# The selected-attention branch of eight decode samples, reordered by phase: keys of both groups first, then values of both groups

## The chip, the cores and the metric

The kernel runs on one core of a Trainium2 chip. The metric is the device time of one execution in microseconds; lower is better. The kernel before has a median of 1252.27 us over three runs (1243.72 to 1252.75).

## The reference

One layer of a hybrid decoder is run for a prompt of 512 tokens and for eight decode samples of four tokens each, with 2048 cached positions behind each sample. The layer is: x plus the output projection of two mixers (a sparse attention called NSA, and an mLSTM), plus cross-attention on a memory, plus a SwiGLU, with RMS norms between. The part that matters here is NSA for the samples, `nsa_attend` in the reference, with 8 heads in 2 key/value groups of width 64:

```python
# compressed branch: scores on compressed keys, softmax, weights on compressed values
# the compressed weights, summed over blocks and heads, rank 32 blocks of 64 tokens; the best 16 are kept
# selected branch: scores on all cached keys, positions outside the kept blocks masked, softmax, values
# window branch: the same over the last 512 positions
out = gate_cmp * o_cmp + gate_slc * o_slc + gate_win * o_win
y = concat(headnorm(out), sigmoid(o) * headnorm(mlstm)) @ w_out
```

The comments in this extract sum up the code. The cached keys and values are gathered through a page table. Every sample has its own pages, so no key or value is shared by two samples.

## The kernel before

All work of a phase of the layer is issued by Python generators that are woven together, and a scheduler in the framework then fixes the order of every engine's instructions from its own estimate of times. The chip runs each engine's list in order; what an instruction waits for is a semaphore of the instruction or transfer that makes its data or frees its buffer.

The stretch that the change touches lies in the middle of the program. In the background runs `compress(1)`, the small MLP that makes compressed values (in the profile the matmuls at L218 to L220 into `bd` and L1296 into `xa`, then L1246 and L1216). Woven into it is the chain `fg`, in which `sample()` is the third part and `open_late()` the last. When `compress(1)` is through, `drain(fg)` runs the rest, and `early_mix()` splits the NSA and mLSTM outputs `oF` into two parts (`mh`, `ml`) for the output projection of the first 272 tokens. That projection is 192 matmuls, in four column chunks of `w_out`, each chunk loaded by three DMAs (L1830, L1832) and split by ScalarE and VectorE into `whi` and `wlo` (L213, L214). A second part of it, on the other 272 tokens, reads `hh` and `hl`.

`sample()` handles the eight samples in two groups `g` of four. For the selected branch, each group goes through these steps:

- weights of the compressed branch: a `quad` of four matmuls against `kcT`, minimum on VectorE, an Exp (L1607) and block sums on VectorE;
- keys: `half` issues four indirect gathers of 512 KB on GpSimd's queue (L573), one for each sample, and each covers half of that sample's keys. `keys` transposes 128 by 512 elements with four TensorE transposes into one of two PSUM banks `tp` (L1517), and `evac` moves them to `kt` (L206 on ScalarE three times of four, L208 on VectorE once);
- selection: a transpose and a matmul (L1624, L1627), the top 16 blocks on VectorE as a mask `mk`, and the mask added to the bias on GpSimd (`M4`, L1642);
- four score chunks: a `quad` (L1527), then VectorE adds the mask and takes the minimum while it moves the scores to `SS` (L1653); between chunks the keys of the next chunk are transposed;
- softmax: four Exp of 128x512 on ScalarE (L1672) and one small one (L1674);
- values: `probs` transposes the weights through the same two `tp` banks to `PTs`, and 64 matmuls (L1693) add weights times gathered values into `po`.

After group 0, and ahead of group 1, `finals_p` finishes the prompt's NSA: the compressed attention is added (L1398, L1401), the squares (L1402) go through a matmul with `bones` (L1407), and a Ln (L1408) and an Exp (L1413) on ScalarE give the norm's factor. The gathered tiles `gat` have eight buffers. A gather waits until the tile that held its buffer has been read for the last time. The gathers go in the order keys(0), values(0), keys(1), values(1), each in two halves. The last two value tiles of group 1 use other buffers and are loaded early.

Of the kernel before, what the change touches and what calls it, by code (L numbers as in the profile page):

```python
# [6 lines left out]
F32 = mybir.dt.float32  # L7
# [29 lines left out]
def body(tc, I, O, stage=99, dbg=None):  # L37
    nc = tc.nc
    with ExitStack() as top:
# [1351 lines left out]
        def finals_p(var):  # L1391
            yield from need(("p", 1))
            var = var[:, :2048].rearrange("p (a b n) -> p a b n", a=2, b=2)
            for j in range(5):
                if j < 4:
                    acc = bank(psp)
                    for v in range(2):
                        nc.tensor.matmul(acc[64 * v:64 * v + 64], vcP[32 * j:32 * j + 32, v], PcT[32 * j:32 * j + 32, v],  # L1398
                                         start=True, stop=True)
                    oj = oF[:, j, :512]  # L1400
                    nc.vector.tensor_tensor(oj, oj, acc, op=OP.add)  # L1401
                    nc.scalar.activation(var[:, j // 2, j % 2], oj, AF.Square)  # L1402
# [12 lines left out]
            yield  # L1415

        def sample():
# [175 lines left out]

            kg = half("cache_k_slc", 0, 0)
            for g in range(2):
                bs = [4 * g + q for q in range(4)]
                rs = sc.tile([128, 4], F32, name="rs4", bufs=2)
                nmn = sc.tile([128, 12], F32, name="nmn", bufs=2)
                kh = half("cache_k_slc", g, 1, range(3))
                yield from need(("c", 0))  # L1600
                pc = bank(psp)
# [15 lines left out]
                nc.vector.scalar_tensor_tensor(blk, edge, 0.5, blk, op0=OP.mult, op1=OP.add)  # L1617
                yield
                kts = [keys(lambda i: kg[q][:, 128 * i:128 * i + 128]) for q in range(2)]
                yield  # L1620
                kts += [keys(lambda i: kg[q][:, 128 * i:128 * i + 128]) for q in range(2, 4)]
                yield
                p = bank(ptp)
# [12 lines left out]
                nc.vector.match_replace(out=ia, in_to_replace=t8[:, 8:16], in_values=ia, imm_value=-BIG)  # L1636
                mk = sc.tile([128, 32], F32, name="mk")
                nc.vector.memset(mk, 0.0)
                nc.vector.tensor_scalar(mk[:, 1:31], ia, -0.5 * BIG, BIG, op0=OP.is_ge, op1=OP.mult)
                M4 = sc.tile([128, 4, 128], F32, name="M4")  # L1640
                for i in range(4):
                    nc.gpsimd.tensor_tensor(M4[:, i].rearrange("p (j r) -> p j r", r=4),  # L1642
                                            B0[:, i].rearrange("p (j r) -> p j r", r=4),
                                            mk[:, :, None].to_broadcast([128, 32, 4]), op=OP.add)
                kh += half("cache_k_slc", g, 1, (3,))
                yield
                yield
                yield
                SS = sc.tile([128, 2080], F32, name="SS")
                for c in range(4):  # L1650
# [4 lines left out]
                    if c == 3:  # L1655
                        break
                    src = kg if c == 0 else kh
# [17 lines left out]
                nc.vector.tensor_reduce(rs[:, 1:2], bs5[:, 5:10], axis=AX.X, op=OP.add)  # L1675
                nx = 2 * g
                vl = half("cache_v_slc", g, 1, range(4 - nx))
                yield
                yield
                if nx:  # L1680
                    yield from need("free")
                    vl += half("cache_v_slc", g, 1, range(4 - nx, 4), True)
                PT_ = probs(lambda i: SS[:, 128 * i:128 * i + 128])
                yield
                po_ = bank(ppo)
                for c in range(4):
                    vg = vh if c < 2 else vl
                    if c < 3:
# [7 lines left out]
                    if c == 0:  # L1696
# [3 lines left out]
                        nc.vector.tensor_copy(PN_, p[:32, 0:128])  # L1700
                    if c == 2 and g == 0:
                        kg = half("cache_k_slc", 1, 0)
                    yield
# [5 lines left out]
                if g == 0:  # L1709
                    yield from finals_p(sc.tile([128, 2080], F32, name="SS"))  # L1710
            pop("sc")
# [874 lines left out]
```

## Time and profile before

| | before |
|---|---|
| three runs, us | 1243.72, 1252.75, 1252.27 |
| median, us | 1252.27 |
| the profiled execution: time, us | 1244.16 |
| the profiled execution: span, us | 1242.4 |
| TensorE busy, share of the span | 95% |
| granted TensorE clock, mean | 0.972 |

The profiled execution is close to the fastest of the three runs; the two others lie some 8.5 us above it. The stretch in question begins near 500 us of the span and ends near 630 us. Times in the rows below are microseconds from the start of the span.

### The profile page before, as it was taken

How to read it: one execution, taken by the hardware profiler on the slowest of the kernel's cores; microseconds unless marked ns; L12 is line 12 of the kernel's file. 1: busy time of each engine (PE TensorE's matmuls, PEld its weight loads, DVE VectorE, ACT ScalarE, POOL GpSimd, SP SyncE). 2: the span in 40 equal slices, each digit the busy share in tenths (PEclk: the TensorE clock that was granted, in tenths of full speed). 3: DMA queues.
4: the chain of work that ended last, by engine and by line, in shares of the span. 5: the costliest groups of instructions: out<-in, count | busy, mean ns of one | idle time of the engine just before them, and what ended most of it. 6: DMA issues, size and time to landing. Idle time of an engine off the chain costs nothing.

```text
span 1242.4 us, 24591 instructions
## 1 busy us (share of the span) xinstructions
PE 1174.2 (95%) x9220; PEld 1066.4 (86%) x9220; DVE 830.3 (67%) x1901; ACT 615.7 (50%) x1418; POOL 564.0 (45%) x686
## 2 busy tenths in 40 slices
PE   7999999899997989988899998999999999999996
PEld 5998999588885879846699977599899999999996
DVE  6336683567887787544566575544987887878874
ACT  5235665745646434474543233433575565565452
POOL 1013353566766366442243100034796586486442
PEclk9998999989997989998899999999999999999998
DMA  7324240141253184585468399650023322322411
GB/s 232 102 53 104 86 152 1 53 135 43 74 175 115 57 294 152 176 276 154 122 168 179 111 221 278 233 169 2 1 100 105 103 94 96 118 94 77 137 52 73
DMA packets 141769, 154.30 MB, mean 124 GB/s; under 512 B 17449, under 2 KB 123689, under 8 KB 141394
## 3 DMA queue, kind: packets, MB, share of 16 engines
q1 hardware_dynamic: 131922, 119.17, 32.1%
q0 software_dynamic: 9728, 33.56, 8.3%
q8 instruction: 73, 1.20, 0.4%
q14 instruction: 46, 0.38, 0.1%
HBM read 141.67 MB, written 13.12 MB: 125 GB/s over the span
## 4 chain that ended last, share of the span: by engine, by line
PE 53%; DVE 7%; DMA 5%; ACT 2%; issue 1%; POOL 1%; SPq 1%; POOLq 0%; DVEq 0%; ACTq 0%
PE xc L2260 7%; PE xa L2260 7%; PE bd L2260 6%; PE tp L2260 5%; PE bd L218 3%; PE bd L220 3%; PE bd L219 3%; PE xa L1296 2%; DMA wraw<-in_w_out 2%; DMA mkv<-in_cache_mem_k 2%; PE tp L1517 1%; PE bd L2159 1%; PE xc L218 1%; PE xc L219 1%; PE xc L220 1%
## 5 line engine op out<-in xcount | busy, mean ns | idle before, releaser
L214 POOL TENSOR_TENSOR al<-fraw,ah 128x512 fp32r<-128x512 f32 (+1 forms) x104 | 127.1, 1224 | 146.8 <-ACT ah L213 118.9
L213 ACT ACTIVATE whi<-wraw 128x1024 fp32r<-128x1024 f32 (+3 forms) x74 | 63.0, 890 | 70.1 <-DMA wraw<-in_w_xv 28.4
L214 DVE TENSOR_TENSOR wlo<-wraw,whi 128x1024 fp32r<-128x1024 f32 (+3 forms) x74 | 75.0, 1041 | 31.2 <-ACT whi L213 31.0
L213 ACT ACTIVATE ah<-fraw 128x512 fp32r<-128x512 f32 (+1 forms) x112 | 66.0, 594 | 43.8 <-PE xc L2260 11.8
L218 PE MATMUL bd<-w1h,xh 128*128 128x256 f32 x256 | 82.9, 326 | 0.0
L1198 POOL TENSOR_TENSOR xs<-xf 128x256 f32<-128x256 f32 x64 | 57.3, 902 | 48.5 <-PE xa L1296 29.7
L220 PE MATMUL bd<-w1h,xl 128*128 128x256 f32 x256 | 75.7, 298 | 1.4 <-DVE xl L214 1.4
L219 PE MATMUL bd<-w1l,xh 128*128 128x256 f32 x256 | 76.1, 298 | 0.0
L1296 PE MATMUL xa<-ws,xs 128*128 128x256 f32 x256 | 70.9, 399 | 1.9 <-DVE bq L1469 1.0
L625 POOL TENSOR_SCALAR sb<-sb,rs,gat 128x128 f32<-128x128 f32 (+3 forms) x64 | 46.2, 726 | 56.0 <-DVE rs L624 41.9
L213 ACT ACTIVATE xh<-xf 128x512 fp32r<-128x512 f32 x64 | 40.1, 632 | 43.6 <-DVE xf L1191 19.8
L213 ACT ACTIVATE ah<-sp 128x512 fp32r<-128x512 f32 (+1 forms) x64 | 35.6, 557 | 41.6 <-DVE sp L2200 16.9
L1191 DVE STREAM_TRANSPOSE xf<-cgat 128x512 f32<-128x512 f32 x64 | 44.9, 704 | 15.8 <-POOL xs L1198 15.0
L220 PEld LDWEIGHTS bd<-w1h,xl 128*128 128x128 f32 x256 | 49.1, 192 | 5.4 <-DVE xl L214 2.8
L219 PEld LDWEIGHTS bd<-w1l,xh 128*128 128x128 f32 x256 | 49.8, 195 | 4.3 <-issue 3.0
L214 DVE TENSOR_TENSOR xl<-xf,xh 128x512 fp32r<-128x512 f32 x64 | 48.2, 757 | 7.2 <-ACT xh L213 6.7
L1296 PEld LDWEIGHTS xa<-ws,xs 128*128 128x128 f32 x256 | 45.8, 198 | 8.1 <-issue 3.0
L218 PEld LDWEIGHTS bd<-w1h,xh 128*128 128x128 f32 x256 | 49.5, 195 | 3.7 <-issue 2.2
L219 PE MATMUL bd<-hlo,whi 128*128 128x272 f32 x176 | 52.4, 298 | 0.0
L218 PE MATMUL bd<-hhi,whi 128*128 128x272 f32 x176 | 52.2, 297 | 0.0
L220 PE MATMUL bd<-hhi,wlo 128*128 128x272 f32 x176 | 51.9, 295 | 0.0
L1874 POOL TENSOR_TENSOR acc<-acc,sq 128x272 f32<-128x272 f32 x35 | 31.4, 896 | 34.3 <-ACT sq L1873 33.9
(988 smaller groups left out, 4672.6 us busy)
## 6 DMA issues: line engine op xcount, KB each, us to landing
fraw<-in_w_gate SPq DMA_DIRECT2D x11, 1024.0 KB
fraw<-in_w_up SPq DMA_DIRECT2D x11, 1024.0 KB
fraw<-in_w_down SPq DMA_DIRECT2D x24, 384.0 KB
mkv<-in_cache_mem_k SPq DMA_DIRECT2D x64, 128.0 KB
mkv<-in_cache_mem_v SPq DMA_DIRECT2D x16, 512.0 KB
wraw<-in_w_in SPq DMA_DIRECT2D x8, 512.0 KB
wraw<-in_w_xq SPq DMA_DIRECT2D x4, 1024.0 KB
wraw<-in_w_xk SPq DMA_DIRECT2D x4, 1024.0 KB
```

What stands on the lines that cost most here:

```text
L213: nc.scalar.activation(hi, src, AF.Copy)
L214: (eng or nc.gpsimd).tensor_tensor(lo, src, hi, op=OP.subtract)
L218: nc.tensor.matmul(out, ah, bh, start=first, stop=False, **kw)
L219: nc.tensor.matmul(out, ah, bl, start=False, stop=False, **kw)
L220: nc.tensor.matmul(out, al, bh, start=False, stop=last, **kw)
L625: (nc.vector, nc.gpsimd)[1].tensor_scalar(sb[:, :n], sb[:, :n], rs, gat[:, i, 3 * h + 1 + br:3 * h + 2 + br], op0=OP.mult, op1=OP.mult)
L1191: nc.vector.transpose(xf.rearrange("p a (q i) -> p q a i", q=4), gs[0].rearrange("p (q t a i) -> p t q a i", q=4, t=4, a=4)[:, t])
L1198: nc.gpsimd.tensor_tensor(xs_.rearrange("p c (v j) -> p v c j", v=2), xg[:, 0], xg[:, 1], op=OP.add)
L1296: nc.tensor.matmul(dst[2], ops[2][:, kk], w1s[t][2][:, kk], start=t == 0 and kk == 0, stop=t == 3 and kk == 1, skip_group_check=True)
L1517: nc.tensor.transpose(p[:, 128 * i:128 * i + 128], srcs(i), ident)
L1874: nc.gpsimd.tensor_tensor(acc[hf], acc[hf], sq, op=OP.add)
L2260: nc.tensor.matmul(p[:, :HALF], w[a][:, k], x[b_][:, k], start=first and k == 0 and i == 0, stop=last and k == n - 1 and i == 2, skip_grou ...
```

## The change

Only `sample()` and `finals_p` change. The gathers, transposes, matmuls and exponentials stay the same in number; four Ln and four Exp of 128x512 in `finals_p` become four copies, one Ln and one Exp of 128x2048. The body of `sample()` is cut into `weigh(g)` and `select(g)`, and the two groups go keys, keys, values, values. Group 1's `weigh` and `select` stand between the score chunks of group 0. The scores `SS` get two buffers, and group 1's mask goes into another tile (`W0`). The gathers now go in the order keys(0), keys(1), values(0), values(1). `finals_p` follows the values of group 0, as before.

```diff
@@ finals_p
-                    nc.scalar.activation(vj, p, AF.Ln, bias=eps_t)
+                    nc.scalar.activation(vj, p, AF.Copy)
...
+            nc.scalar.activation(var, var, AF.Ln, bias=eps_t)
+            nc.scalar.activation(var, var, AF.Exp, scale=-0.5)
             for j in range(4):
                 oj, vj = oF[:, j, :512], var[:, j // 2, j % 2]
-                tc.keep_in_program_order(nc.scalar.activation(vj, vj, AF.Exp, scale=-0.5))
@@ sample
+            G, st_ = {}, {}
+            G[0, "k0"] = half("cache_k_slc", 0, 0)
+            G[0, "k1"] = half("cache_k_slc", 0, 1, range(3))
+            for g in range(2):
...
+                if g == 0:
+                    yield from need(("c", 0))
+                    weigh(0)
                 yield
+                kts = [keys(lambda i: G[g, "k0"][q][:, 128 * i:128 * i + 128]) for q in range(2)]
...
+                if g == 0:
+                    select(0)
+                M4 = sc.tile([128, 4, 128], F32, name=("M4", "W0")[g])
...
-                SS = sc.tile([128, 2080], F32, name="SS")
+                SS = sc.tile([128, 2080], F32, name="SS", bufs=2)
                 for c in range(4):
...
+                    if g == 0 and c > 0:
+                        (weigh, select)[c - 1](1)
+                    if c == 2:
+                        if g == 0:
+                            G[1, "k1"] = half("cache_k_slc", 1, 1)
+                        else:
+                            G[0, "v1"] = half("cache_v_slc", 0, 1)
                     if c == 0:
-                        vh = half("cache_v_slc", g, 0)
+                        if g == 0:
+                            G[0, "k1"] += half("cache_k_slc", 0, 1, (3,))
+                            G[1, "k0"] = half("cache_k_slc", 1, 0)
+                        else:
+                            G[0, "v0"] = half("cache_v_slc", 0, 0)
...
-                vl = half("cache_v_slc", g, 1, range(4 - nx))
+                st_[g] = SS, rs
                 yield
+            for g in range(2):
+                SS, rs = st_[g]
+                if g:
                     yield from need("free")
+                    G[1, "v1"] += half("cache_v_slc", 1, 1, range(2, 4), True)
...
+                    if c == 1 and g == 0:
+                        G[1, "v0"] = half("cache_v_slc", 1, 0)
+                    if c == 3 and g == 0:
+                        G[1, "v1"] = half("cache_v_slc", 1, 1, range(2))
```

Lines after the change are numbered higher: L1518 for L1517, L1528 for L1527, L1626 for L1627, L1660 for L1642, L1701 for L1672, L1722 for L1693. The change moves instructions on every engine. Three places follow.

**TensorE, keys of group 1.** Before, at the second score chunk of group 1 (`sp<-kt,Qn` is a `quad`, `tp<-ident,gat` a key transpose, `xc<-mh,whi` and its like are output projection):

```order
L218 MATMUL xc<-mh,whi 128x272
L219 MATMUL xc<-ml,whi 128x272
L1527 MATMUL sp<-kt,Qn 32x512 x4
L1517 MATMUL tp<-ident,gat 128x128 x4
L220 MATMUL xc<-mh,wlo 128x272
```

With the change, from the selection of group 1 (L1626) on, through the last chunk of group 0 and the first two of group 1:

```order
L1626 MATMUL tp<-blk,GS 128x32
L1528 MATMUL sp<-kt,Qn 32x512 x4
L1518 MATMUL tp<-ident,gat 128x128 x8
L1246 MATMUL xc<-w_5309,hid 127x64 x4
L1518 MATMUL tp<-ident,gat 128x128 x8
L1216 MATMUL xc<-ident,ys 128x128 x4
L1518 MATMUL tp<-ident,gat 128x128 x4
L1528 MATMUL sp<-kt,Qn 32x512 x4
L1518 MATMUL tp<-ident,gat 128x128 x16
L1528 MATMUL sp<-kt,Qn 32x512 x4
```

All output-projection matmuls now stand behind the value matmuls of group 0, and all but four behind those of group 1. In the key phase only L1246 and L1216 of `compress(1)` stand between the transposes.

**ScalarE, the norms of `finals_p`.** Before (`pcs` is group 1's `weigh`, `kt` its keys):

```order
L1408 ACT_TABLE_LOAD
L1408 ACTIVATE SS<-tp,eps_t 128x512 x2
L1607 ACT_TABLE_LOAD
L1607 ACTIVATE pcs,rs_6684<-pcs,nmn 128x127
L1408 ACT_TABLE_LOAD
L1408 ACTIVATE SS<-tp,eps_t 128x512
L213 ACTIVATE mh<-oF 128x272 x4
L1408 ACTIVATE SS<-tp,eps_t 128x512
L1413 ACT_TABLE_LOAD
L1413 ACTIVATE SS<-SS 128x512 x3
L206 ACTIVATE kt<-tp 128x512
L1413 ACTIVATE SS<-SS 128x512
```

With the change (`PTs` are the transposed weights of group 1's values):

```order
L1402 ACTIVATE SS<-oF 128x512
L1408 ACTIVATE SS<-tp 128x512
L1758 ACTIVATE jkn,rs_7401<-po_3201 128x128
L1408 ACTIVATE SS<-tp 128x512
L1411 ACT_TABLE_LOAD
L1411 ACTIVATE SS<-SS,eps_t 128x2048
L206 ACTIVATE PTs<-tp 128x512 x2
L1412 ACT_TABLE_LOAD
L1412 ACTIVATE SS<-SS 128x2048
L206 ACTIVATE PTs<-tp 128x512
L213 ACTIVATE mh<-oF 128x272
```

Four table loads are now two, and what stands behind them is group 1's weights for the values, no longer its keys. The softmax of group 0 (L1701), which stood ahead of `finals_p`, now stands among the key evacuations of group 1.

**GpSimd's queue, the gathers.** Before, from the first values of group 0 on:

```order
L573 DMA gat<-in_cache_v_slc,gx 128x1024
L1642 TENSOR_TENSOR M_6046<-B_5476,mk 128x128 x4
L573 DMA gat<-in_cache_v_slc,gx 128x1024
L1198 TENSOR_TENSOR xs<-xf 128x2x2x64
L573 DMA gat<-in_cache_v_slc,gx 128x1024 x2
L1198 TENSOR_TENSOR xs<-xf 128x2x2x64
L573 DMA gat<-in_cache_v_slc,gx 128x1024 x4
L573 DMA gat<-in_cache_k_slc,gx 128x1024 x8
L214 TENSOR_TENSOR ml<-oF,mh 128x272 x4
L573 DMA gat<-in_cache_v_slc,gx 128x1024
L1642 TENSOR_TENSOR M_6809<-B_5476,mk 128x128 x4
L573 DMA gat<-in_cache_v_slc,gx 128x1024 x5
```

With the change, the same stretch:

```order
L573 DMA gat<-in_cache_k_slc,gx 128x1024
L1660 TENSOR_TENSOR M_6048<-B_5476,mk 128x128 x4
L573 DMA gat<-in_cache_k_slc,gx 128x1024
L1198 TENSOR_TENSOR xs<-xf 128x2x2x64
L573 DMA gat<-in_cache_k_slc,gx 128x1024 x2
L1198 TENSOR_TENSOR xs<-xf 128x2x2x64
L573 DMA gat<-in_cache_k_slc,gx 128x1024 x4
L1660 TENSOR_TENSOR W_6421<-B_5476,mk 128x128 x4
L573 DMA gat<-in_cache_v_slc,gx 128x1024 x4
L214 TENSOR_TENSOR ml<-oF,mh 128x272 x2
L573 DMA gat<-in_cache_v_slc,gx 128x1024 x10
```

All value gathers stand behind all key gathers, and behind the mask of group 1 (`W`).

On SyncE, the loads of `w_out`'s first three chunks keep their place; the fourth stood right behind the third, and now stands behind the sample's x, two later `w_out` loads and the first load of `w_xq`.

## Rows read from the trace of the kernel before

**Rows 1.** The profile page, its first two parts: the span, TensorE's busy share in 40 slices of 31 us, in tenths (the stretch in question is slices 18 to 20).

```profile
span 1242.4 us, 24591 instructions
...
PE   7999999899997989988899998999999999999996
```

**Rows 2.** The view by stretches of time. Columns: the stretch, its length, then busy us and instructions of TensorE, its weight loads, VectorE, ScalarE and GpSimd, then the granted TensorE clock as a share of 2.4 GHz, the share of the DMA engines, GB/s.

```profile
552.30:568.00 15.70, 9.26 (x31) 3.67 (x30) 10.96 (x23) 14.45 (x26) 4.75 (x6) 0.67 0.38 135
568.00:582.00 14.00, 14.00 (x114) 13.01 (x114) 4.34 (x12) 2.75 (x4) 5.31 (x8) 1.00 0.86 265
...
595.00:611.00 16.00, 13.49 (x184) 9.50 (x177) 5.99 (x27) 8.57 (x24) 1.75 (x3) 0.79 0.04 10
...
640.00:860.00 220.00, 213.53 (x1679) 188.11 (x1679) 127.82 (x248) 79.44 (x165) 47.17 (x67) 1.00 0.65 178
533.60:627.40 93.80, 78.89 (x695) 57.05 (x695) 47.43 (x119) 53.52 (x108) 26.07 (x31) 0.89 0.60 188
609.70:627.40 17.70, 16.44 (x139) 15.48 (x135) 14.50 (x38) 9.52 (x23) 5.93 (x8) 1.00 0.92 247
```

**Rows 3.** The view of waits, TensorE, 530 to 611 us: instruction and tile, what ended the wait, us in total, times, the longest.

```profile
PE tp L1517 <- ACT kt L206: 6.6, 3, 2.8
PE tp L1517 <- ACT SS L1408: 2.8, 2, 1.6
```

**Rows 4.** The timeline of TensorE: start, us, instruction, and in brackets the idle time before it and what ended that.

```profile
545.64 1.08 PE L1693 MATMUL po<-gat,PTs 128*32 128x128 f32 x32
...
555.01 0.66 PE L1517 MATMUL tp<-ident,gat 128*128 128x128 f32 x4 [1.65 <-ACT SS L1408]
...
560.33 2.12 PE L1517 MATMUL tp<-ident,gat 128*128 128x128 f32 x8 [2.81 <-ACT kt L206]
...
568.42 0.37 PE L218 MATMUL xa<-mh,whi 128*128 128x272 f32 x1
...
569.51 0.29 PE L220 MATMUL xa<-mh,wlo 128*128 128x272 f32 x1
...
571.03 0.29 PE L219 MATMUL bd<-ml,whi 128*128 128x272 f32 x1
571.16 1.03 PE L1517 MATMUL tp<-ident,gat 128*128 128x128 f32 x8
...
588.11 0.43 PE L220 MATMUL bd<-mh,wlo 128*128 128x272 f32 x1
...
594.38 1.06 PE L1527 MATMUL sp<-kt,Qn 128*32 128x512 f32 x8 [0.69 <-ACT kt L206]
...
601.78 1.94 PE L1693 MATMUL po<-gat,PTs 128*32 128x128 f32 x32
...
627.44 0.40 PE L218 MATMUL xa<-hh,whi 128*128 128x272 f32 x1
```

**Rows 5.** The timeline of ScalarE, same columns: the norms of `finals_p`, splits for the output projection, and the softmax of group 1.

```profile
547.13 1.28 ACT L1408 ACT_TABLE_LOAD   x1
548.42 0.69 ACT L1408 ACTIVATE SS<-tp,eps_t 128x512 f32<-128x512 f32 x1
...
554.86 1.38 ACT L213 ACTIVATE mh<-oF 128x272 fp32r<-128x272 f32 x4
...
556.83 1.28 ACT L1413 ACT_TABLE_LOAD   x1
558.12 1.67 ACT L1413 ACTIVATE SS<-SS 128x512 f32<-128x512 f32 x3
559.70 0.58 ACT L206 ACTIVATE kt<-tp 128x512 f32<-128x512 f32 x1
...
563.88 2.00 ACT L213 ACTIVATE whi<-cgat 128x1024 fp32r<-128x1024 f32 x2
...
596.67 0.32 ACT L1674 ACTIVATE SS<-sn,nmn 128x32 f32<-128x32 f32 x1 [2.34 <-DVE nmn L1668]
...
599.11 0.71 ACT L1672 ACTIVATE SS<-SS,bs 128x512 f32<-128x512 f32 x1
```

**Rows 6.** The view by lines, TensorE, 533.5 to 627.4 us, shapes apart: line, operation, tiles, shapes, times, then busy us in all and mean ns of one, and the idle time before.

```profile
L1693 PE MATMUL po<-gat,PTs 128*32 128x128 f32 x224 | 11.8, 304 | 0.0
L1517 PE MATMUL tp<-ident,gat 128*128 128x128 f32 x64 | 11.0, 309 | 9.5 <-ACT kt L206 6.6 <-ACT SS L1408 2.8
...
L1517 PE MATMUL tp<-ident,SS 128*128 128x128 f32 x32 | 6.8, 323 | 0.1
...
L1407 PE MATMUL tp<-SS,bones 128*128 128x512 f32 x8 | 4.4, 632 | 0.0
L1398 PE MATMUL sp<-PcT,vcP 32*64 32x512 f32 x16 | 4.3, 613 | 0.2 <-DVE oF L1401 0.2
```

**Rows 7.** The view of DMA issues in the stretches 568 to 578 and 589 to 593 us: tile and source, queue, times, median us from issue to landing.

```profile
gat<-in_cache_v_slc,gx POOLq DMA_INDIRECT x4, 8.3
...
gat<-in_cache_v_slc,gx POOLq DMA_INDIRECT x2, 5.1
```

**Rows 8.** The chain of waits that ended last, in order of time (start, us, what): the third and fourth chunk of `w_out`.

```profile
570.21 12.30 DMA wraw<-in_w_out
...
583.63 1.23 DVE wlo L214
...
586.18 4.75 DMA wraw<-in_w_out
```

More of the change, by code (lines that the diff above doesn't have):

```diff
@@ L1592, in half, with weigh @@
                 return r
-            kg = half("cache_k_slc", 0, 0)
-            for g in range(2):
+            sel = {}
+            def weigh(g):
                 bs = [4 * g + q for q in range(4)]
[L1597 to L1600, printed above, removed]
+                rs = sc.tile([128, 4], F32, name="rsc")
+                nmn = sc.tile([128, 1], F32, name="nmc")
                 pc = bank(psp)
@@ L1617, in sample, with select @@
                 nc.vector.scalar_tensor_tensor(blk, edge, 0.5, blk, op0=OP.mult, op1=OP.add)
[L1618 to L1622, printed above, removed]
+                sel[g] = pcs, blk
+            def select(g):
+                pcs, blk = sel[g]
                 p = bank(ptp)
@@ L1636, in sample @@
                 nc.vector.match_replace(out=ia, in_to_replace=t8[:, 8:16], in_values=ia, imm_value=-BIG)
-                mk = sc.tile([128, 32], F32, name="mk")
+                mk = sc.tile([128, 32], F32, name="mk", bufs=2)
                 nc.vector.memset(mk, 0.0)
                 nc.vector.tensor_scalar(mk[:, 1:31], ia, -0.5 * BIG, BIG, op0=OP.is_ge, op1=OP.mult)
-                M4 = sc.tile([128, 4, 128], F32, name="M4")
+                sel[g] = mk
+            G, st_ = {}, {}
+            G[0, "k0"] = half("cache_k_slc", 0, 0)
+            G[0, "k1"] = half("cache_k_slc", 0, 1, range(3))
+            for g in range(2):
+                bs = [4 * g + q for q in range(4)]
+                rs = sc.tile([128, 4], F32, name="rs4", bufs=2)
+                nmn = sc.tile([128, 12], F32, name="nmn", bufs=2)
+                if g == 0:
+                    yield from need(("c", 0))
+                    weigh(0)
+                yield
+                kts = [keys(lambda i: G[g, "k0"][q][:, 128 * i:128 * i + 128]) for q in range(2)]
+                yield
+                kts += [keys(lambda i: G[g, "k0"][q][:, 128 * i:128 * i + 128]) for q in range(2, 4)]
+                yield
+                if g == 0:
+                    select(0)
+                M4 = sc.tile([128, 4, 128], F32, name=("M4", "W0")[g])
                 for i in range(4):
@@ L1643, in sample @@
                                             B0[:, i].rearrange("p (j r) -> p j r", r=4),
-                                            mk[:, :, None].to_broadcast([128, 32, 4]), op=OP.add)
-                kh += half("cache_k_slc", g, 1, (3,))
+                                            sel[g][:, :, None].to_broadcast([128, 32, 4]), op=OP.add)
                 yield
-                yield
-                yield
-                SS = sc.tile([128, 2080], F32, name="SS")
+                if g == 0:
+                    yield
+                    yield
+                SS = sc.tile([128, 2080], F32, name="SS", bufs=2)
                 for c in range(4):
@@ L1656, in sample @@
                         break
-                    src = kg if c == 0 else kh
+                    src = G[g, "k0" if c == 0 else "k1"]
                     kts = []
@@ L1663, in sample @@
                             yield
-                    if c == 0:
-                        vh = half("cache_v_slc", g, 0)
+                    if g == 0 and c > 0:
[5 more added lines that the diff above has]
+                            G[0, "v1"] = half("cache_v_slc", 0, 1)
+                    if c == 0:
+                        if g == 0:
+                            G[0, "k1"] += half("cache_k_slc", 0, 1, (3,))
+                            G[1, "k0"] = half("cache_k_slc", 1, 0)
+                        else:
+                            G[0, "v0"] = half("cache_v_slc", 0, 0)
                 nc.vector.tensor_tensor(nmn[:, 1:5], nmn[:, 1:5], slc_, op=OP.add)
@@ L1675, in sample @@
                 nc.vector.tensor_reduce(rs[:, 1:2], bs5[:, 5:10], axis=AX.X, op=OP.add)
-                nx = 2 * g
-                vl = half("cache_v_slc", g, 1, range(4 - nx))
+                st_[g] = SS, rs
                 yield
-                yield
-                if nx:
+            for g in range(2):
+                SS, rs = st_[g]
+                if g:
                     yield from need("free")
-                    vl += half("cache_v_slc", g, 1, range(4 - nx, 4), True)
+                    G[1, "v1"] += half("cache_v_slc", 1, 1, range(2, 4), True)
                 PT_ = probs(lambda i: SS[:, 128 * i:128 * i + 128])
@@ L1686, in sample @@
                 for c in range(4):
-                    vg = vh if c < 2 else vl
+                    vg = G[g, "v0" if c < 2 else "v1"]
                     if c < 3:
@@ L1700, in sample @@
                         nc.vector.tensor_copy(PN_, p[:32, 0:128])
-                    if c == 2 and g == 0:
-                        kg = half("cache_k_slc", 1, 0)
+                    if c == 1 and g == 0:
+                        G[1, "v0"] = half("cache_v_slc", 1, 0)
+                    if c == 3 and g == 0:
+                        G[1, "v1"] = half("cache_v_slc", 1, 1, range(2))
                     yield
@@ L1709, in sample @@
                 if g == 0:
-                    yield from finals_p(sc.tile([128, 2080], F32, name="SS"))
+                    yield from finals_p(sc.tile([128, 2080], F32, name="SS", bufs=2))
             pop("sc")
```

## The prediction, made before the changed kernel had run

> **What bounds the kernel now.** TensorE. The span is 1242.4 us and TensorE is busy in nearly all of it; three slices of 31 us in the middle, 18 to 20, are at 8 tenths, and that is the stretch in question [rows 1]. From the view by stretches the reader sees where the slack is: 640 to 860 us has 213.53 us of work in 220, so nothing is to be gained behind the change and whatever it moves arrives at the end undiminished. Between 533.6 and 627.4 us TensorE is busy 78.89 of 93.8 us: 14.9 us idle, and the granted clock is 0.89 on average. The worst piece is 552.3 to 568 us, with 9.26 busy of 15.7 and a clock of 0.67, that is, largely at 1.2 GHz; 595 to 611 us has 0.79 [rows 2]. The view of waits says for what: 6.6 us for key evacuations on ScalarE (three waits, the longest 2.8) and 2.8 us for the Ln of the norms [rows 3]. The timeline of ScalarE shows that these are one cause: Ln and Exp alternate with table loads of 1.28 us each, group 1's first keys stand behind them, and the evacuation at 559.70 comes only after the three Exp at 558.12 [rows 5]; TensorE then resumes at 560.33 after 2.81 us, and eight transposes take 2.12 us where at full clock they take 1.03 [rows 4]. I end the stretch at 627.44, where the first matmul of the projection's second part (`hh`) stands: behind it the order is almost the same in both kernels.
>
> **The change, part by part.** The orders agree up to 533.6 us, so I build the time from there to the first `hh` matmul.
>
> *Keys of group 1 (phase K).* No projection matmul and no norm stands there any more. TensorE's own work is short, so ScalarE sets the pace: 12 key evacuations at 0.59 are 7.1, group 0's softmax 0.32 + 4 x 0.71 = 3.2, `mh` 1.4, four halves of `whi` at 1.0 are 4.0 [rows 5], 15.7 us together. To that come the turns in which a `quad` waits for the last `kt` and the next transposes wait for a `tp` bank; walking the order row by row with these durations, one turn of about 1 us stands at each of the five quads, and about 3 us where four Exp or the `whi` splits stand ahead of an evacuation. I take 23.4 us. The bounds: 15.7 below, and above what group 1's keys took before, from 555.0 to the end of the last quad at 595.4 = 40.4, less the projection that stood in between. That projection is 96 of its 192 matmuls, between 568.42 and 588.11, at (571.03 - 569.51) / 12 = 0.127 us each [rows 4], 12.2 us, so 28.2.
>
> *Values of both groups, with the norms (phase V).* Work at full clock: eight sets of 16 value matmuls at 1.08 = 8.6, 32 transposes at 1.03 for eight = 4.1 [rows 4], L1398 4.3, L1407 4.4 [rows 6], 21.4 together. The norms move in front of group 1's weights. Four Ln of 0.69, four Exp of 0.56 and four loads of 1.28, 10.1 us of ScalarE [rows 5], become four copies, which hide under TensorE, one Ln and one Exp over 2048 columns, and two loads. No row has 2048 columns: copies of 512 and 1024 columns take 0.58 and 1.0, so 0.4 per further 512, and I put each at 0.6 + 3 x 0.45 = 2.0 (bounds: one call of 512 columns, 0.56, and four of them, 2.8). ScalarE is thus taken for two spells of 1.28 + 2.0 = 3.3 us, with two `PTs` evacuations between; TensorE has about 1.2 us of transposes and the values of one chunk (1.0) to put beside each, so some 2 us of each stay exposed, 4 in all. V = 25.4 us.
>
> The row at 548.42 shows Ln starting 0.01 us after its load has ended [rows 5], so each load that goes is worth 1.28 us, two of them 2.6, and the two that stay cost no more than that. The Trainium skill ("ScalarE: Activation LUTs", section "What ACT_TABLE_LOAD costs") adds a drain and gives about 2.66 us for a switch; by it the two would be worth 5.3. The trace does not agree, and my sum does not use that figure.
>
> *Projection (phase O).* From 609.7 to the first `hh` matmul 17.7 us passed with the other 96 matmuls [rows 2]. The 96 that are no longer used as filler come back here as 12.2 us: this cover is lost in full, and every gain above is net of it. The fourth chunk of `w_out` now stands on SyncE behind the sample's x, two other chunks and a `w_xq` load. Before, a chunk took 4.75 or 12.30 us to arrive [rows 8]; three chunks (144 x 0.127 = 18.3 us of matmuls) run ahead of it, so I count a wait of 1 us (bounds 0 and 8, the difference of the two transfers). O = 30.9.
>
> *Gathers.* Their number is the same, the queue's order is not: all sixteen key gathers go first, then the values. Eight buffers hold them, and a value gather is issued when a key tile has been transposed. Two gathers issued together landed in 5.1 us, four in 8.3 [rows 7]. In my walk the first half of group 0's values is issued at 538 to 545 and used at 557, the second at 550 to 555 and used at about 563, group 1's first half at 560 to 565 and used at 575. Each just arrives: zero, with a margin between 0 and 4 us.
>
> *Clock.* Where the stretch ran below full speed it lost about 9.26 x 0.33 = 3.1 us between 552.3 and 568 and 13.49 x 0.21 = 2.8 us between 595 and 611 [rows 2]. K will have TensorE waiting for ScalarE throughout, so part of V will start at 1.2 GHz. I take 5 us (bounds 0 and 13, V wholly at a clock of 0.67).
>
> Sum: 533.6 + 23.4 + 25.4 + 30.9 + 5 = 618.3, against 627.4: 9.1 us earlier. The profiled execution took 1244.16, so 1235 on its scale. The median of the runs shown, 1252.27, lies 8.1 above the profile; two of three runs are up there. On that scale the forecast is 1243. I name the middle, **1239**.
>
> **The rivals.**
>
> *Faster: the clock holds and ScalarE keeps up.* K = 20 (the 15.7 us and one turn for each chunk), no loss to the clock: 533.6 + 20 + 25.4 + 30.9 = 609.9, 17.5 us earlier, 1227 on the profile's scale. For it: the wait of 2.81 us behind the norms, right ahead of the slow transposes at 560.33 [rows 4], is gone from the keys. Against it: K leaves TensorE idle more than a third of the time.
>
> *No change: the idle time moves.* K at its upper bound (28.2) and V slowed to a clock of 0.79 (32.2): 533.6 + 28.2 + 32.2 + 30.9 = 624.9, 2.5 us earlier, 1242; at 0.67 throughout V is 37.9 and the time 1247. What speaks for it is the trace itself: 568 to 582 us, where the projection filled the gaps between the keys, has 14.00 busy of 14.00 us at a clock of 1.00, while the keys without filler just ahead ran at 0.67 [rows 2]; the change takes that filler away. The Trainium skill ("TensorE: Matmul & The Clock Gate", section "HAM oscillation — how this bites in real kernels") describes the same: pieces of matmul work parted by waits each start at the low rate again, so a kernel pays for the transition many times. By that rule, the likeliest outcome would be this rival; the trace agrees as far as the two stretches named go, and I leave the forecast ahead of it only because the value matmuls and transposes of V stand close behind one another.
>
> *Slower: the value gathers are exposed.* Buffers of the keys come free only as K ends, so if the second half of group 0's values, then both halves of group 1's arrive late, TensorE waits three times for 8.3 us, 25 in all: 1260 on the profile's scale. It decides where the last gather of a half is issued less than 8.3 us before its use; my margins are 0 to 4 us. Against it: before, the largest waits of this stretch are for ScalarE and none of them for a gather [rows 3].
>
> That the order does not change is excluded by the lists of the two kernels.
>
> **How the numbers follow.** Forecast 0.45 (3 to 12 us gained), faster rival 0.27, no change 0.17, slower rival 0.11. The runs of before spread over 9 us, 0.7%, so 1% (12.5 us) is about what a measurement can tell. Over 1% faster: the faster rival and the top of the forecast, 0.32. Over 1% slower: the exposed gathers, 0.11. Within 1%: 0.57. The range leaves out the extremes of the two outer rivals: from 1225 (faster rival on the profile's scale) to 1257 (no change at the upper scale, with a partly exposed gather).
>
> **What would show it.** In the profile after: key transposes at 533 to 557 us with waits `<- ACT kt`, no projection matmul among them; two table loads in `finals_p`, each followed by an activation of about 2 us, with TensorE waiting on `PTs`; 192 projection matmuls in one piece, starting near 582 to 587, with at most a short wait for the fourth `whi`; the first `hh` matmul at 610 to 622. Wrong would be: waits of the value matmuls on `DMA gat`; the piece 533 to 557 lasting over 28 us; a long wait of the projection for `w_out`; or a stretch behind 640 us that is no longer nearly full.

## The result, and the profile after

The changed kernel has a median of 1240.47 us over seven runs (1236.38 to 1245.15), the kernel before 1249.16 us over seven (1243.72 to 1252.75). The ratio is 0.9942, with a 95% interval of 0.9919 to 0.9965: about 7 us faster, 0.6%. That is clear of zero, though less than the 1% that the prediction called measurable. A second series (`after_again` below) gave 0.9918 (0.9888 to 0.9948).

The profiled execution itself is hardly shorter, 1243.24 us against 1244.16. To see why, I read a **local time**, from a store that both kernels issue right ahead of the changed stretch (the first of the two `nxt` stores at L1305 that begin after 503 us; L1306 in two of the experiments) to the first `hh` matmul. First the timeline of SyncE's queue before, then the same after, then TensorE's timeline after.

```profile
510.91 0.53 SPq L1305 DMA_DIRECT2D nxt<-cur  x1
```

```profile
514.24 0.53 SPq L1305 DMA_DIRECT2D nxt<-cur  x1
```

```profile
544.32 1.66 PE L1528 MATMUL sp<-kt,Qn 128*32 128x512 f32 x8 [2.63 <-ACT kt L206]
545.91 3.31 PE L1518 MATMUL tp<-ident,gat 128*128 128x128 f32 x16
...
583.65 1.08 PE L1722 MATMUL po<-gat,PTs 128*32 128x128 f32 x32 [3.14 <-ACT PTs L206]
...
588.94 0.37 PE L218 MATMUL xa<-mh,whi 128*128 128x272 f32 x1
...
621.01 0.39 PE L218 MATMUL xa<-hh,whi 128*128 128x272 f32 x1
```

Before, the local time is 627.44 [rows 4] - 510.91 = 116.5 us; after, 621.01 - 514.24 = 106.8. So 9.8 us are won in the stretch. In this execution 3.3 us had been lost ahead of it, where TensorE's lists of the two kernels agree, and 5.5 behind it.

The view by stretches splits the local time. First the whole before. Then after: up to the end of group 0's last quad (538.0), keys of group 1, a piece of these, values, projection, the whole, and the stretch behind.

```profile
510.91:627.44 116.53, 100.35 (x864) 74.84 (x863) 59.45 (x147) 64.17 (x129) 37.33 (x45) 0.91 0.61 190
```

```profile
514.24:538.00 23.76, 23.13 (x180) 18.61 (x179) 13.66 (x39) 11.14 (x23) 11.24 (x14) 1.00 0.60 188
538.00:561.90 23.90, 17.75 (x128) 11.17 (x125) 14.62 (x36) 17.11 (x36) 11.98 (x14) 0.93 0.81 282
544.30:549.57 5.27, 4.91 (x25) 2.68 (x25) 2.56 (x6) 3.44 (x7) 1.87 (x2) 0.68 0.75 279
561.90:591.05 29.15, 24.35 (x327) 13.76 (x328) 10.14 (x30) 19.10 (x34) 7.80 (x9) 1.00 0.58 188
591.05:621.01 29.96, 29.86 (x243) 28.41 (x242) 22.51 (x48) 16.41 (x35) 10.49 (x13) 1.00 0.75 214
514.24:621.01 106.77, 95.10 (x872) 71.96 (x871) 60.93 (x151) 63.76 (x128) 41.51 (x48) 0.98 0.68 216
640.00:860.00 220.00, 214.47 (x1659) 188.44 (x1658) 125.78 (x243) 76.33 (x158) 41.86 (x63) 0.98 0.62 173
```

The matmuls are the same but for eight small ones of L1817 that now fall into the stretch (864 and 872 in the rows). TensorE was busy 100.35 us and idle 16.2 before, busy 95.10 and idle 11.7 after. The idle time fell by 4.5 us; the busy time fell by 5.3, since the granted clock rose from 0.91 to 0.98. In this pair of executions half of the gain is the clock, which before lay at 0.67 in the keys of group 1 [rows 2] and here at 0.93. The two repeats below read 113.4 and 109.7 us, with 98.35 and 96.96 us busy: 3.7 us won, 2.4 of it idle time. The mean of both pairs, 6.8 us, agrees with the ratio.

The waits of TensorE in the stretch, first those before that [rows 3] does not show, then after:

```profile
PE sp L1527 <- ACT kt L206: 1.7, 2, 1.0
PE po L1786 <- DVE oF L208: 1.3, 1, 1.3
PE sp L1786 <- ACT oF L206: 1.1, 1, 1.1
PE sp L1718 <- DVE nmn L1653: 0.8, 1, 0.8
PE sp L1786 <- DVE po L1722: 0.5, 1, 0.5
```

```profile
PE po L1722 <- ACT PTs L206: 3.7, 2, 3.1
PE sp L1528 <- ACT kt L206: 3.0, 2, 2.6
PE tp L1518 <- ACT kt L206: 1.5, 2, 0.8
```

The 2.8 us for the Ln are gone, and of the 6.6 for key evacuations behind it 1.5 are left. But before quads of group 1 the wait grew from 1.7 to 3.0 us (the softmax of group 0 is ahead of the evacuation), and 3.7 now stand before value matmuls of group 1, behind the norms. Added up, the waits in keys and values were 12.4 us before and are 11.5 after; in the repeats 11.9 and 12.0. This idle time moved and hardly fell. What fell are the 3.7 us at the end of the samples, where L1718 completes their outputs and L1786 transposes x: after, these matmuls stand among the projection's, and no wait for them is left (3.2 and 0.5 us in the repeats).

ScalarE's timeline shows the two new waits:

```profile
542.98 0.71 ACT L1701 ACTIVATE SS<-SS,bs 128x512 f32<-128x512 f32 x1
543.59 0.19 ACT L1701 ACTIVATION_READ_ACCUMULATOR SS<-SS,bs 128x1 f32 x1
543.69 0.58 ACT L206 ACTIVATE kt<-tp 128x512 f32<-128x512 f32 x1
...
579.22 0.59 ACT L1408 ACTIVATE SS<-tp 128x512 f32<-128x512 f32 x1
579.82 1.28 ACT L1411 ACT_TABLE_LOAD   x1
581.12 2.00 ACT L1411 ACTIVATE SS<-SS,eps_t 128x2048 f32<-128x2048 f32 x1
583.02 1.06 ACT L206 ACTIVATE PTs<-tp 128x512 f32<-128x512 f32 x2
584.11 1.28 ACT L1412 ACT_TABLE_LOAD   x1
585.40 1.91 ACT L1412 ACTIVATE SS<-SS 128x2048 f32<-128x2048 f32 x1
```

The quad at 544.32 waits 2.63 us until the evacuation at 543.69 is over, which came behind four Exp. From it to the end of the sixteen transposes after it the granted clock is 0.68, and they take 1.66 and 3.31 us. The values at 583.65 wait 3.14 us for `PTs` at 583.02, which came behind a load and the Ln.

### The profile page after: what moved, and what is told of

It reads as the page before. It is cut to its first block, busy times and chain, and to the rows that moved or that the text cites. A ratio compares the mean times of both kernels' runs of the same rounds, so it can differ in the third digit from the quotient of the medians.

```text
span 1241.5 us, 24581 instructions
## 1 busy us (share of the span) xinstructions
PE 1174.3 (95%) x9220; PEld 1066.7 (86%) x9220; DVE 841.2 (68%) x1901; ACT 612.4 (49%) x1414; POOL 558.6 (45%) x686
## 4 chain that ended last, share of the span: by engine, by line
PE 49%; DVE 8%; ACT 3%; DMA 2%; issue 2%; SPq 1%; POOL 1%; POOLq 0%; DVEq 0%; ACTq 0%
PE xc L2291 7%; PE xa L2291 7%; PE bd L2291 5%; PE tp L2291 5%; PE bd L220 3%; PE bd L219 3%; PE bd L218 3%; DVE sp L2231 1%; DMA mkv<-in_cache_mem_k 1%; PE xa L1296 1%; PE tp L1518 1%; PE bd L2190 1%; PE xa L218 1%; PE xa L219 1%; PE xa L220 1%
## 5 line engine op out<-in xcount | busy, mean ns | idle before, releaser
L2231 DVE TENSOR_TENSOR sp<-fraw 128x512 f32<-128x512 f32 (+1 forms) x32 | 47.8, 1494 | 0.2
```

The costliest lines, as they stand in the source:

```text
L2231: nc.vector.tensor_tensor(o, a, b, op=op)
```

## The experiments

| run | what differs | ratio to before, 95% interval | local, us | behind, us |
|---|---|---|---|---|
| before, `before_again` | | 0.9988 (0.9971 to 1.0006) | 116.5, 113.4 | 615.0, 616.0 |
| the change, `after_again` | | 0.9942 (0.9919 to 0.9965), 0.9918 (0.9888 to 0.9948) | 106.8, 109.7 | 620.5, 617.1 |
| `e1_one_ln_only` | before + one Ln | 0.9990 (0.9967 to 1.0012) | 119.5 | 615.0 |
| `e2_old_norms` | change, old norms | 0.9931 (0.9903 to 0.9960) | 107.2 | 617.3 |
| `e10_early_select_only` | before + early selection | 0.9976 (0.9958 to 0.9994) | 111.5 | 616.3 |
| `e9_late_select`, `e9_again` | change, late selection | 0.9939 (0.9915 to 0.9963), 0.9973 (0.9953 to 0.9993) | 114.9, 106.5 | 613.5, 622.8 |
| `e3_softmax_spread` | change, Exp spread | 0.9922 (0.9894 to 0.9950) | 105.5 | 616.4 |
| `e4_pts_on_vector` | change, `PTs` by VectorE | 0.9947 (0.9922 to 0.9972) | 110.5 | 616.8 |
| `e5_gathers_late` | change, values' gathers later in the source alone | 0.9904 (0.9876 to 0.9933) | 111.0 | 617.0 |
| `e6_filler_back` | change, projection from k = 4 | 0.9979 (0.9963 to 0.9995) | 117.3 | 616.5 |
| `e7_filler_and_spread` | e3 and e6 | 0.9912 (0.9884 to 0.9940) | 104.3 | 617.3 |

"Behind" is the span less the time of the first `hh` matmul. Local times are of one execution each; two executions of one program lie 3 us apart in two pairs, and 8 in the third.

**Which part of the change does it: the norms?** `e1_one_ln_only` takes only the part of the change in `finals_p`, `e2_old_norms` leaves out just that.

```diff
-                    nc.scalar.activation(vj, p, AF.Ln, bias=eps_t)
+                    nc.scalar.activation(vj, p, AF.Copy)
...
+            nc.scalar.activation(var, var, AF.Ln, bias=eps_t)
+            nc.scalar.activation(var, var, AF.Exp, scale=-0.5)
...
```

> Before, with the change of the norms alone (four copies, one Ln, one Exp); groups and gathers stay in the old order. Measured by the ratio to before and by the local time, from the first store of nxt near 511 us to the first hh matmul (before 116.5 us, changed kernel 106.8 us). Theory A, the phase order makes the gain because it takes the norms out from ahead of group 1's keys: local 113 to 117, ratio 0.997 to 1.001, since the Ln and the Exp still stand among the keys' evacuations. Theory B, the fewer table loads make it: local 106 to 110, ratio 0.992 to 0.995.

> The changed kernel with the old norms (Ln for each of the four, Exp for each of the four); order by phase kept. The scheduler leaves two table loads also here, since no other Exp falls between. Theory A (order): local 106 to 108, ratio 0.992 to 0.996, as the changed kernel. Theory B (one Ln): the gain goes, local 112 to 116, ratio 0.997 to 1.001.

The one Ln alone gave no gain that can be measured (0.9990), and the change without it is as good as with it (0.9931). In the old order a block of 1.28 + 2.00 us still stands ahead of group 1's keys, and the longest wait for it is no shorter than that for the alternating loads, 3.14 us against 2.81 (timeline of ScalarE, then of TensorE, `e1_one_ln_only`):

```profile
551.57 1.28 ACT L1411 ACT_TABLE_LOAD   x1
552.87 2.00 ACT L1411 ACTIVATE SS<-SS,eps_t 128x2048 f32<-128x2048 f32 x1
554.77 1.06 ACT L206 ACTIVATE kt<-tp 128x512 f32<-128x512 f32 x2
...
588.51 1.06 ACT L213 ACTIVATE whi<-wraw 128x1024 fp32r<-128x1024 f32 x1 [2.75 <-DMA wraw<-in_w_out]
589.48 0.58 ACT L206 ACTIVATE kt<-tp 128x512 f32<-128x512 f32 x1
```

```profile
555.40 1.11 PE L1518 MATMUL tp<-ident,gat 128*128 128x128 f32 x4 [3.14 <-ACT kt L206]
...
590.11 1.07 PE L1528 MATMUL sp<-kt,Qn 128*32 128x512 f32 x8 [3.64 <-ACT kt L206]
...
595.80 0.65 PE L1719 MATMUL sp<-vcn,po 127*32 127x128 f32 x8 [4.63 <-DVE nmn L1654]
```

Both runs fit theory A by their ratios; the local 119.5 of the first lies above its range. The last two waits, 8.3 us together, go far to explain it. ScalarE's split of `w_out` at 588.51 waited for its load, and the key evacuation that the quad needs stood behind it; VectorE's pass over the scores (L1654) stood behind its part of the next split. So this profile does not tell what the one Ln would win where the loads are in time.

Two table loads instead of four are left in both runs, and in `e10_early_select_only` as well: with the one Ln, with the new order, and with the early weights, no Exp of group 1 stands between two Lns.

**The selection or the phases?** `e10_early_select_only` takes the early selection alone into the kernel before, `e9_late_select` takes it out of the change.

```diff
...
+                    if g == 0 and c > 0:
+                        (weigh, select)[c - 1](1)
...
```

> Before, with group 1's compressed weights and selection moved into group 0's score chunks, and nothing else; the groups go one after the other and the gathers in the old order. It also takes group 1's Exp from between the Lns, so two table loads are left without the one Ln. Theory A, this part of the change is worth something by itself but the norms still stand ahead of group 1's keys: local 110 to 114 (before 113.4 and 116.5), ratio 0.995 to 1.000. Theory B, it is the larger part of the gain and the phase order adds little: local 106 to 109, ratio 0.990 to 0.994.

> The changed kernel, with group 1's compressed weights and selection again at the head of group 1's keys instead of inside group 0's score chunks; phase order and norms kept. Theory A, the selection is a chain of small VectorE steps that lies beside the keys in either place, and the first score of group 1 that needs the mask comes late enough: local 106 to 110, as the changed kernel (106.8 and 109.7 in two executions). Theory B, the first chunk's mask is late, so scores, quads and keys of group 1 stand behind it: local 111 to 115.

> The phase order with the late selection once more, since its first profile read 114.9 us locally with two long falls of the clock, and 613.5 behind, while its ratio (0.9939) is as good as the changed kernel's. Theory A, the late selection costs 3 us or more of local time each time (its wait of 2.7 us on the weights, and what the clock loses after it): local 111 or more. Theory B, the first profile was an unlucky one in the clock: local 106 to 110.

The early selection by itself gives 0.9976, some 3 us (theory A), with the norms still ahead of group 1's keys; the phases without it 0.9939 and 0.9973, 3 to 8 us. The early selection does not make all of the gain. The phases without it are as good as the change in one series and less in the other, so what the early selection adds to them stays open. The single profiles of the second kernel can't tell more: the same program read 114.9 and 106.5 us locally. In the first of them TensorE ran at 1.2 GHz far longer, and its clock was 0.90 against 0.97 (view by stretches, first execution, then second):

```profile
507.72:622.57 114.85, 102.97 (x872) 76.09 (x871) 62.05 (x151) 64.47 (x128) 41.40 (x48) 0.90 0.65 201
```

```profile
511.94:618.43 106.49, 95.20 (x872) 73.09 (x871) 61.42 (x151) 64.21 (x128) 41.16 (x48) 0.97 0.69 217
```

Busy time differs by 7.8 us and idle time by 0.6, with 872 matmuls recorded in both. So theory B of `e9_again` holds for the local time: the first reading was the clock's. The wait of 2.7 us for the weights was there both times.

**What the two new waits cost.** `e3_softmax_spread` puts each Exp of group 0 behind the last key evacuation of a chunk; `e4_pts_on_vector` moves `PTs` to VectorE, for group 1 alone.

```diff
...
+                        if g == 1 and q == 3:
+                            with tc.issue_after(last_ev[0].ins):
+                                soft0(c)
...
```

> The changed kernel, with group 0's softmax no longer as one block ahead of a key evacuation: each of its four Exp stands behind the last key evacuation of one of group 1's chunks. In the changed kernel TensorE waits 2.63 us at the first quad of group 1 and its clock falls right after. Theory A, that wait is the block of Exp: it falls under 1 us, the fall of the clock goes too, local 103.5 to 105.5. Theory B, ScalarE is full in the key phase and the 2.8 us of Exp come back as waits of later chunks: local 106 to 107.5.

```diff
-                evac(PT_, four_t(srcs).rearrange("p (i r) -> p i r", i=4))
+                p = four_t(srcs).rearrange("p (i r) -> p i r", i=4)
+                if dve:
+                    nc.vector.tensor_copy(PT_, p)
+                else:
+                    evac(PT_, p)
...
```

> The changed kernel, with group 1's transposed weights evacuated by VectorE instead of by ScalarE, where they stood behind the Ln and the Exp of the norms (waits of 3.14 and 0.53 us before value matmuls). Theory A, these waits are what the values lose and the projection follows the values: local 103 to 104. Theory B, the projection does not wait for the values but for the chain Ln, Exp, scaling of oF, ml; taking two evacuations of 0.5 us out of that chain gives 1 us: local 105.3 to 106.3, and the wait shows before the first matmul with ml.

Spreading the Exp brought the wait before quads from 3.0 to 0.6 us, but that before key transposes rose to 3.0 (1.5 and 2.3 in the two profiles of the change). The local time of 105.5 is at the edge of theory A, 1.3 us under the lower one of the change, and the ratio lies between the change's two: no gain that can be measured. Moving `PTs` fitted neither theory. The wait only changed its engine, because VectorE has to scale `oF` (L1415) behind the Exp, and the last `PTs` stood behind that (waits of TensorE, then VectorE's timeline, `e4_pts_on_vector`):

```profile
PE po L1726 <- DVE PTs L1538: 2.5, 2, 1.9
...
PE xa L218 <- ACT mh L213: 1.7, 1, 1.7
PE po L1726 <- DMA gat<-in_cache_v_slc,gx: 1.5, 1, 1.5
```

```profile
580.93 3.26 DVE L1415 SCALAR_TENSOR_TENSOR oF<-oF,gh,SS 128x512 f32<-128x512 f32 x4 [2.78 <-ACT SS L1412]
584.11 0.68 DVE L1538 COPY PTs<-tp 128x512 f32<-128x512 f32 x1
```

**The slower rival.** `e5_gathers_late` puts the issue of group 0's value gathers, in the source, behind all scores of group 1.

```diff
...
                 st_[g] = SS, rs
+                if g:
+                    G[0, "v0"] = half("cache_v_slc", 0, 0)
+                    G[0, "v1"] = half("cache_v_slc", 0, 1)
```

> The changed kernel, with group 0's value gathers issued only behind the last score chunk of group 1 instead of behind its first and third: this prices the slower rival. In the changed kernel they are issued from 542.1 to 550.7 and from 554.7 to 560.9 us, and the values start at 561.9 without a wait for them. In the list of GpSimd's instructions their order does not change much (each still waits for a key tile to be read), but all of them now stand behind the keys in priority. Theory A, the value gathers had a margin near zero and the issue order is set by the buffers: local 106 to 109, waits on gat of 0 to 3 us. Theory B, they become exposed: two batches of four at 8.3 us each, local 115 or more, TensorE waiting for DMA gat.

> The changed kernel once more, unchanged, on the chip of the others. Its first profile gained 9.8 us up to the first hh matmul and gave 5.5 back behind it (620.5 us from there to the end, against 615.0 before), and had lost 3.3 before the changed stretch began. Theory A, what lies ahead of and behind the stretch is variation from execution to execution: local 106 to 108 again, the part behind it 615 to 618. Theory B, the change costs something later: the part behind 619 to 621 again.

The edit moved nothing: the instructions of every engine stand in the same order in the traces of `e5_gathers_late` and `after_again`. The second gather of the batch goes out 33.35 us behind the store in `after_again` (510.11), and 33.34 in `e5_gathers_late` (509.37). Their timelines of GpSimd:

```profile
543.46 0.94 POOL L573 DMA_INDIRECT gat<-in_cache_v_slc,gx  x1 [4.51 <-PE tp L1518]
```

```profile
542.71 0.94 POOL L573 DMA_INDIRECT gat<-in_cache_v_slc,gx  x1 [4.51 <-PE tp L1518]
```

So this is a third execution of the changed kernel (0.9904, local 111.0), not a test, and later gathers were not tried. TensorE waited 2.6 us for a gather here, and 1.8 us in `after_again`; the first profile had no such wait (waits of TensorE, `after_again`, then `e5_gathers_late`):

```profile
PE po L1722 <- DMA gat<-in_cache_v_slc,gx: 1.8, 1, 1.8
```

```profile
PE po L1721 <- DMA gat<-in_cache_v_slc,gx: 2.6, 1, 2.6
```

The margin of the changed kernel is thus about zero, and what is missed is 0 to 2.6 us in three executions. `after_again` read 109.7 us locally, above its theory A, and 617.1 behind, within it.

**The lost cover.** `e6_filler_back` starts the projection's first two chunks at the mLSTM half (k = 4), whose `mh` and `ml` are there early.

```diff
-  ... split_w(won[c]), two(2 * c)) for c in range(2)], mixh, KT, residual, dbk, group=2, hfs=(0,)),
+  ... split_w(won[c]), two(2 * c)) for c in range(2)], mixh, KT, residual, dbk, group=2, hfs=(0,), k0=4),
```

> The changed kernel, with the output projection's first two chunks starting at the mLSTM half of the contraction (k 4 to 7 first, which needs no NSA norm) instead of at the NSA half. So 48 of its matmuls can stand between the last keys and the values again, as filler. Tests what the lost cover costs. Theory A, TensorE's idle time in the values (4.8 us there, 6.1 in the keys) is what the filler can use and the projection behind the values gets shorter by what was filled: local 101 to 104.5, no fall of the clock in this stretch. Theory B, the projection is bound by the chain Ln, Exp, scaling, ml and by the fourth chunk of w_out, and filler ahead of it only lengthens the keys: local 106 to 108.

> Both the spread softmax and the projection starting at the mLSTM half. Theory A, the two remove different idle time and add up: local 99 to 103 and a ratio of 0.985 to 0.990 to before. Theory B, the same idle time is counted twice, or the third chunk of w_out is late: local 104 to 106, ratio as the spread softmax alone (0.992).

The filler went where it was meant to, and the local time rose to 117.3: neither theory had that. The projection behind it, now shorter, caught up with the loads of `w_out`: ScalarE's `oF` evacuations stood behind splits that waited for these loads, and TensorE behind them (`e6_filler_back`: waits of TensorE; then SyncE's queue; then, from the chain of waits, the last DMA of a chunk):

```profile
PE sp L1817 <- ACT oF L206: 8.7, 2, 4.7
```

```profile
594.38 1.82 SPq L1802 DMA_DIRECT2D cgat<-in_x_sample  x1
596.31 1.26 SPq L1861 DMA_DIRECT2D wraw<-in_w_out  x2
```

```profile
599.63 10.86 DMA wraw<-in_w_out
```

These loads stand on SyncE behind the sample's x (594.38), whose buffer is a value tile of group 1, so they can't be issued before the values end. With the softmax spread as well (`e7_filler_and_spread`) they were issued from 591.47 and the wait was 1.7 us; why the two differ so much was not tried. Its 0.9912 fits theory B. Theory A's 0.985 to 0.990 is outside what was measured.

**Does the change cost something behind?** The first profile after had 620.5 us there against 615.0, and most others of that order 616.4 to 617.3, so 2 us seemed to be real.

> The kernel before once more, for the spread of the readings: the local time (first store of nxt near 511 us to the first hh matmul, 116.5 in the first profile) and the part behind it (615.0). Theory A, the phase order costs about 2 us behind the stretch, since the seven profiles with that order and a normal tail have 616.4 to 617.3 there: here 614.5 to 615.5 again, local 115 to 119. Theory B, the part behind is variation: 616 to 618 here.

The kernel before read 616.0, and two executions of one program (`e9`) 613.5 and 622.8. The traces tell more. From the first matmul into `bd` that reads `xhT` on, every engine's list is the same in all these runs. The time from `hh` to there is 263.5 to 264.2 us in the four profiles of the old order and 262.7 to 265.8 in the ten of the new (means 263.9 and 264.2). So of the 2.0 us between the means behind (615.6 and 617.5) 0.3 arise where the lists differ. The rest arises over one and the same list, which took 350.7 to 358.0 us: most of it is variation from execution to execution.

## Why the prediction was right, point by point

**The time.** 1239 was forecast and 1240.47 measured; 9.1 us were to be gained, 8.7 came by the medians and 7.2 by the ratio. The likeliest case came, in part by luck. 1239 was the middle between 1235, on the scale of the profile, and 1243; the profile itself took 1243.24. And in that profile the parts of the sum missed by +0.5 us (K), +3.75 (V), -0.9 (O), -5 (the clock, whose loss lies in K's figure) and +1.4 (a piece ahead of the sum, below), which together make -0.3.

**Phase K.** 23.4 us forecast, 23.9 measured (538.0 to 561.9). The largest turn was where the walk of the order had it, behind the block of Exp (2.63 us, about 3 forecast); the others were under 1 us each.

**Phase V.** 25.4 us and most of the 5 for the clock were forecast, 29.15 measured at a clock of 1.00. The sum holds, its parts do not. The exposed spells were 3.7 us (4 forecast), and Ln and Exp over 2048 columns took 2.00 and 1.91 (2.0 forecast). The Ln began 0.02 us behind its load (581.12 after 579.82 + 1.28), so the load's price of 1.28 held. It is not the 2.66 us that the Trainium skill gives ("ScalarE: Activation LUTs", section "What ACT_TABLE_LOAD costs"). But the sum of work left out some 2.5 us of small matmuls (L1727, L1735, L1749, L1817), and 1.1 us went to pauses among the value matmuls near 571 us with no releaser in the trace.

**Phase O.** 30.9 forecast, 29.96 measured; no wait for the fourth chunk. The cover for the keys is lost, as forecast, but the projection now covers something else: the end of the samples, where 3.7 us of waits stood before. The prediction did not see these. In `e6_filler_back` the cover could not be had back, since `w_out` was then late; with the softmax spread (`e7_filler_and_spread`) the local time was 1.2 us under that of the spread alone, less than two executions differ.

**Clock.** The 5 us were put into V. In the first profile the only fall came in K (0.93 there, 1.00 in V and O), where it cost about 2 us in the quad and the sixteen transposes. This was the mis-sized term in this execution. In `after_again` it fell in V as well (view by stretches, values):

```profile
558.04:588.50 30.46, 25.51 (x317) 14.56 (x321) 10.04 (x29) 19.11 (x34) 7.36 (x8) 0.89 0.61 182
```

With 0.93 in K that is some 4 us, most of it in V, close to the forecast: 25.51 x 0.11 = 2.8 and 17.53 us busy in K x 0.07 = 1.2. One execution does not give this term. The Trainium skill ("TensorE: Matmul & The Clock Gate", section "HAM oscillation — how this bites in real kernels") has pieces of matmul work start at the low rate after waits. The trace agrees in K, at the quad behind the wait of 2.63 us; behind the longer wait of 3.14 us in V the first profile shows 1.00.

**What the sum had not.** The orders do not agree up to 533.6 us, as the prediction says: TensorE's lists part at 523.9, where the early weights come in. From the store to the end of group 0's last quad 22.4 us passed before and 23.8 after. The prediction began behind it and missed these 1.4 us.

**Gathers.** "Each just arrives, zero" held in the first profile of the change; 1.8 and 2.6 us were waited in its two others, and 0.6 to 1.6 in variants of it. A wait of value matmuls for `gat` was one of the prediction's signs of being wrong. It came, at a tenth of the slower rival's price: 2.6 us at most, not three batches at 8.3.

**Reason for the gain.** The prediction gave it to the norms leaving the way of group 1's keys. That is not shown. No run moved the norms alone, and the waits in keys and values show what the rival "no change" said, idle time that moves: 12.4 and 11.9 us before, 11.5 and 12.0 after. What fell is the idle time at the end of the samples, by 3.7 and 2.7 us, and TensorE's busy time, by 5.3 in the first pair and 1.4 in the second. `e10_early_select_only` wins some 3 us with the norms where they were, though with two loads fewer. What the experiments do show is that the one Ln is not the reason (`e1_one_ln_only`, `e2_old_norms`). Of the two loads that go, worth 2.6 us in the text, none needs the merged Ln: they go by the order or the early weights as well.

## What to carry to other kernels

A latency chain on one engine (table load, Ln, load, Exp) costs what stands behind it in that engine's list; merging it won nothing here that could be measured, and moving it moved the wait to what stands behind it now. So add up the waits of the whole stretch, before and after, before a gain is credited to the one wait that is gone. Before giving up filler on TensorE, look for what bounds the piece that gets it back: here a weight load, queued behind a transfer that waits for a buffer. An edit of the source that a scheduler reorders may move nothing: compare the lists of the two traces before the run is read as a test. And where the clock falls in a stretch, compare busy time and granted clock of several executions of one program before a single profile is believed.

## What was not expected of the hardware

One program gave 102.97 and 95.20 us of TensorE busy time for the same stretch in two executions, at granted clocks of 0.90 and 0.97. A profile's clock loss thus differs from execution to execution, here by as much as the whole change is worth. What sets it between executions stays open.
